# Two transformer-like blocks on one core: weights of the experts split by half chunks in a written order, last tiles and LRU weights rearranged

## The chip, the cores and the metric

The kernel runs on 1 core of one Trainium2 chip. The metric is the device time of one execution in microseconds (us). The core's engines have a queue each and run in order: TensorE (PE; its weight loads are shown as PEld), VectorE (DVE), ScalarE (ACT), GpSimd (POOL), and SyncE (SP), which here issues most DMAs. GpSimd's queue issues the others, all indirect ones among them.

## The reference, cut to what matters

Input x is 1024 tokens by 1024, in float32. A first block (gated mixing, a state-space branch, cross attention) ends in a layer norm. The second block is:

```python
h = rms_norm(x, norm_mix)
lru_in, lru_gate, q, k, v, g_lru, g_attn = split(h @ w_in)
hr = rg_lru(causal_depthwise_conv(lru_in, conv_w, conv_b), ...)   # two block-diagonal gates, a scan over tokens
y_lru = (gelu(lru_gate) * hr) @ w_lru_o
o_attn = diff_attention(q, k, v, cos, sin, ...)   # 8 heads, mask: key chunk of 64 <= query chunk of 64
mixed = sigmoid(g_lru) * y_lru + sigmoid(g_attn) * (o_attn @ w_attn_o)
x = x + mixed @ w_out
x = x + memory_cross_attention_2(x, mem, ...)
x = x + hierarchical_moe(rms_norm(x, norm_ffn), ...)   # 32 experts, top 2 of one group of 8

def expert_block(xb, e):
    gu = xb @ w_gate_up[e]                              # 1024 -> 2 x 512
    return (silu(gu[:, :512]) * gu[:, 512:]) @ w_down[e]  # 512 -> 1024
```

## The kernel before, in words

Every large product is made of three matmuls (`mm3`, lines 174 to 176): each operand is split into a high half in fp32r, copied by ScalarE (`act`, line 154), and a low half, the difference, made by VectorE (`tt`, line 166); `split` does both, and the product is high by high, high by low, low by high. Lines 154, 158, 162, 163 and 166 are helpers that all stages share, so rows are told apart by the names of their tiles.

The order of instructions on each engine is set when the program is built: a scheduler takes them by priority and by the time at which it estimates each to be ready. `high_priority` and `behind` move a block's priority, and `issue_after(i)` keeps a block's instructions on i's engine behind i. A tile of a pool with n buffers waits until the one n allocations before it was last read.

The stages in order, with rough times from the trace:

- The first block (0 to 370 us) and `ln1` (to 465): for 8 tiles of 128 tokens, output product, layer norm, RMS norm, transposes, split into `xnh`, `xnl` (`transpose_split`, line 949). The norm's sum of squares is ScalarE's, its reciprocal roots are GpSimd's (`rsqrt`, line 179). `self.ln_end` holds the last tile's square and scaling; the splits of the memory's transposed input `mh`, `ml` wait for both.
- `lru` (465 to 720): for 8 chunks of 128 channels an input projection (`proj`, tile `pj`, 1024 tokens), a convolution, a gate projection, two small gate products (`pg`), and elementwise work up to a scan. `stream` allocates the split weights (`wh`, `wl`, 4 buffers) and issues load and split right where the projection is traced. `mem2` is a generator that projects the memory's keys and values (`w_ckv`, same 4 buffers) in the gaps; its PSUM pool has one buffer, shared by product and transposes. `attn_const` comes last.
- `attention` (720 to 1440): it begins with the tables `rot` for keys (1) and queries (0), on GpSimd, and the masks `ma`, `mb`. Each query tile and half head has score products (lines 1487, 1488) and one product that adds -2^100 on masked columns (line 1490): ma is 128 by 128, mb 128 by 384, of which 256 columns are used, all fp32r.
- `out_proj` (to 1620) and the mixer (to 1890): output product, memory cross attention as steps s1 to s10 on 8 tiles (`step(n)` works on several tiles at once), routing (`route`). The last tile is alone in its batch: s8 (output product, residual, square), s9 (transposes for the router, then `rows`: x3d and out are written), s10. Between them the first loads of experts' weights are issued as memory comes free (`moe_ahead`): a ring of 1 + 6 + 6 raw buffers (pools RX, RA, RB) of 128 x 4 x 512.
- `moe` (1890 to the end): each expert has 6 chunks of weights of 1 MB, 4 of `w_gu` and 2 of `w_dn`. It takes at most 96 tokens of its list: an indirect load `gather` of rows of 4 KB from x3d into `xg` (3 buffers), transposes and split (`x_parts`), `up` 4 times, `gated`, `a_parts` (transposes and split of the activations), `down` twice, each with a scaling `y` by VectorE, and an indirect `scatter` that adds the rows to out. That is 72 matmuls of 512 columns and 12 transposes an expert. `parts` splits a whole chunk (3 buffers). The loop, lines 2302 to 2325, traces up 0, the activations of the expert before, up 1 and 2, the next expert's `x_parts`, the gather for e + 4, up 3, `gated`, then the two `down` of the expert before and its scatter. `w()` takes the next chunk; from the 78th load on (LIM) the ring no longer uses RB, so it has 7 buffers. A loop for lists over 96 rows stands at the end.

Of the kernel before, what the change touches and what calls it, by code (L numbers as in the profile page):

```python
# [11 lines left out]
F32 = mybir.dt.float32  # L12
# [12 lines left out]
EPS = 1e-6  # L25
# [5 lines left out]
NY = 3  # L31
N0 = 2
CT = 8
NRA, NRB, NRX = 6, 6, 1
OVAT = 8
LIM = 78
# [93 lines left out]
class Model:  # L130
# [37 lines left out]
    def split(self, hi, lo, src, eng=None):  # L168
        self.act(hi, src, AF.Copy)
        self.tt(lo, src, hi.bitcast(F32), OP.subtract, eng)  # L170

    def mm3(self, ps, l, r, start, stop):
        mm = self.nc.tensor.matmul
        mm(ps, l[0], r[0], start=start, stop=False)  # L174
        mm(ps, l[0], r[1], start=False, stop=False)  # L175
        mm(ps, l[1], r[0], start=False, stop=stop)  # L176
# [767 lines left out]
    def transpose_split(self, src, PT, hi, lo):  # L944

        for q in range(2):
# [3 lines left out]
            self.split(hi[:, 4 * q:4 * q + 4], lo[:, 4 * q:4 * q + 4], pt)  # L950
# [6 lines left out]
    def ln1(self):  # L957
# [4 lines left out]
        with self.pool("lnw1") as LW, self.pool("lny", side="right") as NW, self.pool("ln", side="right") as N, self.pool("lnps", bufs=2, space=PSUM) as PO, \  # L962
# [3 lines left out]
            def finish():  # L966
                i, xn = last.pop(0)
                self.transpose_split(xn, PT, self.xnh[:, :, i * 128:(i + 1) * 128],
                                     self.xnl[:, :, i * 128:(i + 1) * 128])
# [18 lines left out]
            for i in range(8):  # L988
# [17 lines left out]
                r = N.tile([128, 2, 512], F32, name="r", tag="r")  # L1006
                st = N.tile([128, 2, 6], F32, name="st", tag="st", bufs=2)
                for n in range(2):
                    self.stt(r[:, n], xr[:, n * 512:(n + 1) * 512], ALPHA, ps[:, n], OP.mult, OP.add)
                    nc.vector.bn_stats(out=st[:, n], in_=r[:, n])  # L1010
                if i < 6:
                    nxx.append(load_x(i + 2))
                mv = N.tile([128, 8], F32, name="mv", tag="mv", bufs=2)
                nc.vector.bn_aggr(out=mv[:, 0:2], in_=st)
                self.ts(mv[:, 2:3], mv[:, 1:2], LN_EPS, OP.add)
                self.rsqrt(mv[:, 3:4], mv[:, 2:3], 1)
                r1 = r.rearrange("p a b -> p (a b)")
                self.ts(r1, r1, mv[:, 0:1], OP.subtract, mv[:, 3:4], OP.mult)
                x1 = N.tile([128, 1024], F32, name="x1t", tag="x1t")
                self.tt(x1, r1, lg, OP.mult)  # L1020
                self.tt(x1, x1, lb, OP.add, nc.vector if i == 7 else nc.gpsimd)
                nc.gpsimd.dma_start(out=self.x1[i], in_=x1)
                xn = N.tile([128, 1024], F32, name="xnt", tag="xnt", bufs=2)
                sq = self.act(xn, x1, AF.Square, accum=mv[:, 4:5])
                self.ts(mv[:, 5:6], mv[:, 4:5], 1.0 / 1024, OP.mult, EPS, OP.add)
                self.rsqrt(mv[:, 6:7], mv[:, 5:6], 1)
                xs = self.stt(xn, x1, mv[:, 6:7], nm, OP.mult, OP.mult)
# [9 lines left out]
    def lru(self):  # L1037
# [9 lines left out]
        with self.pool("lru") as T, self.pool("m2") as M, \  # L1047
                self.pool("pj2", bufs=2, space=PSUM) as PJ, self.pool("pg2", bufs=3, space=PSUM) as PG, \
                self.pool("pm2", bufs=1, space=PSUM) as PM:
            beside = self.mem2(W, M, PM)  # L1050
# [5 lines left out]
            def proj(src, w=None):  # L1056

                w = w or self.stream(W, src, [128, 8, 128])
# [19 lines left out]
            first = [proj(A["w_li"][c], None if c else self.w0) for c in range(2)]  # L1078
# [4 lines left out]
            ahead = next(first[1])  # L1083
            for c in range(8):
                xc = nxt
                if c < 7:
                    nxt = conv(c + 1, ahead if c == 0 else [*proj(A["w_li"][c + 1])][1])
                ps = [*proj(A["w_lgate"][c])][1]
# [11 lines left out]
                for g, t in ((1, ti), (0, tr)):  # L1100
                    for h in range(2):
# [3 lines left out]
                        self.act(t[:, z], p, AF.Tanh, bias=self.hb[:, 2 + 8 * g + c:3 + 8 * g + c], scale=0.5)  # L1105
                next(beside, None)
# [20 lines left out]
            with self.tc.issue_after(self.ln_end[1].ins):  # L1127
                self.attn_const(self.at0)
# [21 lines left out]
    def attn_const(self, T):  # L1150
# [13 lines left out]
        self.sub, self.lamn, self.gcol, self.grow = sub, lamn, gcol, grow  # L1164

    def attention(self):
# [4 lines left out]
        with self.pool("at1") as T1, self.pool("at") as T, \  # L1171
# [3 lines left out]
            sub, lamn, gcol, grow = self.sub, self.lamn, self.gcol, self.grow  # L1175
            rot = {}
            for j in (1, 0):
                t = T1.tile([128, 8, 2, 16], F32, name=f"rot{j}")
                g1 = grow[:, j:j + 1, 0:8].to_broadcast([128, 8, 8])
                g2 = grow[:, j:j + 1, 8:16].to_broadcast([128, 8, 8])  # L1180
                self.tt(t[:, :, 0, 0:8], self.ropec, g1, OP.mult, nc.gpsimd)
                self.tt(t[:, :, 0, 8:16], self.ropes, g1, OP.mult, nc.gpsimd)
                self.tt(t[:, :, 1, 0:8], self.ropes, g2, OP.mult, nc.gpsimd)
                nc.gpsimd.tensor_scalar(out=t[:, :, 1, 0:8], in0=t[:, :, 1, 0:8], scalar1=-1.0, scalar2=None, op0=OP.mult)
                self.tt(t[:, :, 1, 8:16], self.ropec, g2, OP.mult, nc.gpsimd)
                rot[j] = t

            ma = T.tile([128, 128], F32R, name="ma")
            mb = T.tile([128, 384], F32R, name="mb")
            nc.gpsimd.memset(ma.bitcast(F32), 0.0)  # L1190
            nc.gpsimd.memset(mb.bitcast(F32), 0.0)
# [667 lines left out]
    def mixer_tiles(self, x2, XX, xxp, PQ, PT, wcq, wrt, wqp):  # L1859
# [89 lines left out]
        def s8(i, halves=(0, 1)):  # L1949
# [8 lines left out]
            if 1 not in halves:  # L1958
                return
# [525 lines left out]
```

## Time and profile before

| | |
|---|---|
| median of 3 runs | 2520.61 us (2520.1 to 2521.86) |
| profiled execution, its own time | 2518.23 us |
| its span, first to last instruction | 2516.5 us |
| granted TensorE clock, mean | 0.982 |
| PE busy, share of the span | 94% |
| VectorE, ScalarE, GpSimd | 70%, 50%, 20% |
| moved by DMA | 394.29 MB |

The rows come from one profiled execution. Times are us, unless marked ns; L166 is line 166. A matmul's row shows its time through the array with a modelled end; matmuls follow each other more closely than that, so the pace is read from their starts. "Idle before" or a bracket gives the engine's idle time ahead of an instruction and whose end released it.

### The profile page before, as it was taken

What the parts mean: (1) busy time and instruction counts of PE and PEld (TensorE: products, weight loads), DVE (VectorE), ACT (ScalarE), POOL (GpSimd) and SP (SyncE); (2) the same over time, 40 slices, a digit from 0 to 9 for tenths busy, and PEclk for the clock granted to TensorE, in tenths of its full rate; (3) what the DMA queues carried; (4) which work ended last, traced back from release to release, by engine and by line L of the source; (5) the groups of instructions that cost most, each with busy time, mean ns of one, the idle gap of its engine ahead of it and who ended that gap; (6) DMA issues with size and microseconds to landing.
All of it is one profiled execution on the core that took longest, in us unless ns stands there. A gap on an engine that the chain in (4) does not pass through costs nothing. (4 is left out here: it accounts for less than half of the span.)

```text
span 2516.5 us, 34506 instructions
## 1 busy us (share of the span) xinstructions
PE 2364.3 (94%) x13016; PEld 1951.4 (78%) x13016; DVE 1772.8 (70%) x3221; ACT 1246.2 (50%) x1850; POOL 504.8 (20%) x362
## 2 busy tenths in 40 slices
PE   8999989989999999999899899999988999988887
PEld 6888868777889898898798778888876777666665
DVE  9667767676775666666666744236658999988887
ACT  5344532453645545455455522124435777766664
POOL 1011114100021021021121100000002333355542
PEclk9999999999999999999999999999988999999999
DMA  6322353312111111110111466532158998999995
GB/s 222 95 70 63 116 187 115 122 69 91 63 68 55 64 35 40 62 51 34 53 49 40 141 204 220 173 138 80 72 217 308 376 373 306 366 338 336 334 338 183
DMA packets 103834, 394.29 MB, mean 157 GB/s; under 512 B 14129, under 2 KB 33073, under 8 KB 79089
## 3 DMA queue, kind: packets, MB, share of 16 engines
q1 hardware_dynamic: 85008, 335.18, 37.8%
q0 software_dynamic: 18656, 56.88, 7.1%
q8 instruction: 104, 1.70, 0.3%
q14 instruction: 66, 0.53, 0.1%
HBM read 339.07 MB, written 61.31 MB: 159 GB/s over the span
## 5 line engine op out<-in xcount | busy, mean ns | idle before, releaser
L166 DVE TENSOR_TENSOR wl<-raw,wh 128x2048 fp32r<-128x2048 f32 (+2 forms) x310 | 566.0, 1839 | 120.0 <-ACT wh L154 119.6
L154 ACT ACTIVATE wh<-raw 128x2048 fp32r<-128x2048 f32 (+2 forms) x310 | 479.6, 1556 | 290.4 <-PE pj L175 87.3
L2248 POOL DMA_INDIRECT out<-y,lsti x32 | 175.2, 5475 | 331.4 <-DVE y L162 281.3
L175 PE MATMUL pg<-wl,xh 128*96 128x512 f32 x512 | 205.6, 402 | 30.1 <-DVE wl L166 29.9
L174 PE MATMUL pj<-wh,xnh 128*128 128x256 f32 x768 | 221.5, 289 | 3.2 <-ACT pc L154 2.7
L176 PE MATMUL pj<-wh,xnl 128*128 128x256 f32 x768 | 217.7, 284 | 0.0
L175 PE MATMUL pj<-wl,xnh 128*128 128x256 f32 x768 | 217.4, 283 | 0.0
L176 PE MATMUL pg<-wh,xl 128*96 128x512 f32 x512 | 201.7, 394 | 0.0
L174 PE MATMUL pg<-wh,xh 128*96 128x512 f32 x512 | 198.3, 396 | 1.0 <-ACT wh L154 1.0
L174 PEld LDWEIGHTS pj<-wh,xnh 128*128 128x128 f32 x768 | 145.4, 189 | 6.2 <-ACT pc L154 4.8
L175 PEld LDWEIGHTS pj<-wl,xnh 128*128 128x128 f32 x768 | 145.5, 189 | 0.0
L176 PEld LDWEIGHTS pj<-wh,xnl 128*128 128x128 f32 x768 | 145.3, 189 | 0.0
L179 POOL TENSOR_TENSOR ss<-ss,mhalf 128x4 f32<-128x4 f32 (+1 forms) x68 | 74.2, 1092 | 343.6 <-DVE ss L163 254.0
L175 PEld LDWEIGHTS pg<-wl,xh 128*96 128x96 f32 x512 | 82.8, 162 | 76.4 <-DVE wl L166 44.5
L154 ACT ACTIVATE e<-sc,st,ss 128x1024 f32<-128x1024 f32 (+7 forms) x128 | 105.6, 829 | 64.5 <-DVE st L158 47.6
L174 PEld LDWEIGHTS pg<-wh,xh 128*96 128x96 f32 x512 | 82.9, 162 | 37.3 <-ACT wh L154 1.4
L174 PE MATMUL pj<-xnh,wh 128*128 128x512 f32 x256 | 103.4, 405 | 7.3 <-ACT wh L154 7.0
L176 PEld LDWEIGHTS pg<-wh,xl 128*96 128x96 f32 x512 | 83.1, 162 | 32.7
L175 PE MATMUL pj<-xnl,wh 128*128 128x512 f32 x256 | 102.4, 401 | 1.3 <-DVE xnl L166 1.3
L174 PE MATMUL pg<-xnh,wh 128*128 128x512 f32 x256 | 103.1, 403 | 0.4 <-ACT kv L154 0.3
L176 PE MATMUL pj<-xnh,wl 128*128 128x512 f32 x256 | 101.9, 400 | 0.3 <-DVE wl L166 0.3
L176 PE MATMUL pg<-xnh,wl 128*128 128x512 f32 x256 | 102.1, 399 | 0.0
(997 smaller groups left out, 6429.5 us busy)
## 6 DMA issues: line engine op xcount, KB each, us to landing
raw<-in_w_gu SPq DMA_DIRECT2D x128, 1024.0 KB, 7.7
raw<-in_w_dn SPq DMA_DIRECT2D x64, 1024.0 KB, 9.6
raw<-in_w_out SPq DMA_DIRECT2D x16, 512.0 KB, 4.5
ta<-tg POOLq DMA_DIRECT2D x32, 256.0 KB, 2.4
t<-ta SPq DMA_DIRECT2D x14, 512.0 KB, 4.3
raw<-in_w_ga SPq DMA_DIRECT2D x12, 512.0 KB, 3.5
raw<-in_w_v SPq DMA_DIRECT2D x12, 512.0 KB, 3.4
xraw<-in_xT SPq DMA_DIRECT2D x8, 512.0 KB, 8.9
```

What stands on the lines that cost most here:

```text
L154: return self.nc.scalar.activation(out=out, in_=in_, func=func, **kw)
L166: return (eng or self.nc.vector).tensor_tensor(out=out, in0=a, in1=b, op=op)
L174: mm(ps, l[0], r[0], start=start, stop=False)
L175: mm(ps, l[0], r[1], start=False, stop=False)
L176: mm(ps, l[1], r[0], start=False, stop=stop)
L179: self.nc.gpsimd.tensor_tensor(out=out, in0=in_, in1=self.mhalf[:, :w], op=OP.pow)
L2248: return nc.gpsimd.indirect_dma_start(out=self.out, out_offset=bass.IndirectOffsetOnAxis(ap=u["row"], axis=0), in_=u["y"], in_offset=None, ...
```

## The change

It has these parts:

- `ln1`: the last tile's chain gets a high priority; `ln_end` is now the last split, so the splits of the memory's input come behind that.
- `lru`: `proj` takes weights streamed one projection ahead. In `mem2` the two token halves share one PSUM tile, and the transposes use the pool of the gate products. `attn_const` comes in the second of 8 chunks and makes the keys' table and the masks too.
- `unit_qk`: mask operands in bf16, 64 columns.
- Mixer: the gather buffers are filled by GpSimd; the last tile's residual and square go by halves, with a sum of the two squares; its `rows` come behind that sum; `wco` has a pool of its own, left after the last tile's output product, where a pool `moe1` with two more raw buffers and the split buffers opens.
- `moe`: chunks are split by halves (128 x 2 x 512, 4 buffers), each 4 halves ahead of its matmuls. Transposes follow a given matmul; their splits, `gated` and the scalings of y, now ScalarE's, follow a given half's split. LIM is gone: the ring has 15 buffers throughout.

```diff
-NRA, NRB, NRX = 6, 6, 1
+NP = 4
+NRA, NRB, NRX, NRP = 6, 6, 1, 2
-LIM = 78
...
@@ ln1
+                with self.tc.high_priority(URGENT) if i == 7 else nullcontext():
                     r = N.tile([128, 2, 512], F32, name="r", tag="r")
...
-            self.ln_end = sq, xs
             finish()
-            finish()
+            self.ln_end = finish()
...
@@ lru
+            def ahead():
+                if srcs:
+                    ws.append(self.stream(W, srcs.pop(0), [128, 8, 128]))
-            def proj(src, w=None):
-                w = w or self.stream(W, src, [128, 8, 128])
+            def proj(w=None):
+                w = w or ws.pop(0)
+                ahead()
...
+                if c == 1:
+                    with self.tc.issue_after(self.ln_end[1].ins):
+                        self.attn_const(self.at0)
...
@@ attn_const, attention
+        self.rotation(T, 1)
+        self.ma = ma = T.tile([128, 128], BF, name="ma")
+        self.mb = mb = T.tile([128, 64], BF, name="mb")
-            for j in (1, 0):
+            self.rotation(T1, 0)
...
@@ unit_qk
-                    nc.tensor.matmul(base[:, o + n - 256:o + n], ma, mb[:, 128:384] if i == 0 else mb[:, 0:256],
-                                     start=False, stop=True)
+                    end = 128 if i == 0 else o + n
+                    nc.tensor.matmul(base[:, end - 64:end], ma, mb, start=False, stop=True)
...
@@ mem2
-            pt = PS.tile([128, 2, 128], F32, name="pt", tag="pj")
+            pt = PG.tile([128, 2, 128], F32, name="pt", tag="pg")
+            pair = PS.tile([128, 2, 2, 128], F32, name="pj", tag="pj")
-                ps = PS.tile([128, 2, 128], F32, name="pj", tag="pj")
+                ps = pair[:, t]
...
@@ mixer_tiles
+            if len(halves) == 1:
+                n = halves[0]
+                q = slice(512 * n, 512 * n + 512)
+                self.tt(x2[i][:, q], x2[i][:, q], ps[:, n], OP.add)
+                self.act(s[:, q], x2[i][:, q], AF.Square, accum=(rs3[:, i:i + 1], self.ms[:, 0:1])[n])
                 return
...
+                if i == 7 and q:
+                    last = self.tt(rs3[:, 7:8], rs3[:, 7:8], self.ms[:, 0:1], OP.add)
-            rows(i)
+            with tc.issue_after(last.ins) if i == 7 else nullcontext():
+                rows(i)
...
                 s8(7, (1,))
+                wcp.__exit__(None, None, None)
+                self.partsp = self.pool("moe1")
+                self.PARTS = self.partsp.__enter__()
+                self.moe_ahead((self.PARTS, NRP), NRP)
...
-                            nc.vector.memset(t, 0.0)
+                            nc.gpsimd.memset(t, 0.0)
...
@@ moe
-                self.ts(u["y"][:, q], p, u["gate"], OP.mult)
+                self.act(u["y"][:, c * 512:c * 512 + 512], u["pd", c], AF.Copy, scale=u["gate"])
...
+            def ahead(n):
+                if n < len(work):
+                    if n % 2 == 0:
+                        self.moe_ahead()
+                        raws.append(self.moe_raw.pop(0))
+                    ready.append(parts(raws[-1], n % 2))
...
+            for n in range(NP):
+                ahead(n)
+            for n, (f, e, c, k) in enumerate(work):
+                u = U[e]
+                m = f(u, c, k, ready[n][0:2])
+                last = ready[min(n + NP, len(work)) - 1]
+                with tc.issue_after(m.ins):
+                    if f is up and (c, k) == (0, 1) and e > 0:
+                        a_turn(U[e - 1])
+                    if f is up and (c, k) == (1, 1) and e < 31:
+                        x_turn(U[e + 1])
+                with tc.issue_after(last[2].ins), tc.issue_after(last[3].ins):
+                    if f is up and (c, k) == (0, 1) and e > 0:
+                        a_split(U[e - 1])
+                    if f is up and k == 3:
+                        gated(u, c)
+                    if f is up and (c, k) == (1, 1) and e < 31:
+                        x_split(U[e + 1])
+                    if f is down and k == 1:
+                        scaled(u, c)
...
+                ahead(n + NP)
+                if f is up and (c, k) == (1, 1) and e < 28:
+                    with tc.issue_after(put.ins) if e > 1 else nullcontext():
+                        gather(U[e + 4])
+                if f is down and (c, k) == (1, 1):
+                    put = scatter(u)
...
```

`work` lists for each expert its 8 half chunks of `up` and then the 4 half chunks of the expert before's `down`.

## Rows read from the trace of the kernel before

**Rows 1.** Part 1 of the page: busy us, share of the span, instructions of each engine.
```profile
PE 2364.3 (94%) x13016; PEld 1951.4 (78%) x13016; DVE 1772.8 (70%) x3221; ACT 1246.2 (50%) x1850; POOL 504.8 (20%) x362
```
**Rows 2.** Stretches by stage: us, busy (instructions) PE PEld DVE ACT POOL, PEclk, DMA share, GB/s.
```profile
465.00:720.00 255.00, 240.29 (x1122) 197.66 (x1123) 190.97 (x186) 134.19 (x158) 12.80 (x20) 0.97 0.24 81
...
1620.00:1890.00 270.00, 252.50 (x1433) 215.02 (x1431) 144.43 (x325) 102.32 (x205) 18.71 (x21) 0.97 0.35 131
1890.00:2503.00 613.00, 577.21 (x2690) 401.05 (x2690) 554.71 (x444) 416.45 (x323) 251.06 (x62) 0.99 0.94 333
```
**Rows 3.** The same view, two stretches of the MoE between starts of scatters.
```profile
1949.25:2091.32 142.07, 142.07 (x676) 100.30 (x675) 139.16 (x120) 106.42 (x82) 48.93 (x17) 1.00 1.01 374
2200.24:2403.22 202.98, 181.76 (x842) 124.38 (x841) 174.91 (x132) 131.07 (x101) 110.91 (x21) 1.00 0.97 336
```
**Rows 4.** Waits of 2200 to 2400: us in total, times, longest.
```profile
ACT xh L154 <- PE pt L2205: 45.4, 10, 4.5
...
PE pg L175 <- DVE wl L166: 19.6, 19, 1.6
```
**Rows 5.** Timeline of PE at the first and last products of the experts: start, us.
```profile
1896.20 0.90 PE L2205 MATMUL pt<-ident,xg 96*128 96x96 f32 x4 [3.61 <-DMA xg<-x3d,lsti]
...
2502.74 0.39 PE L176 MATMUL pd<-wh,ahl 128*96 128x512 f32 x1
```
**Rows 6.** Groups by form, 2200 to 2400: busy us, mean ns, idle before.
```profile
L166 DVE TENSOR_TENSOR wl<-raw,wh 128x2048 fp32r<-128x2048 f32 x60 | 135.5, 2284 | 16.5 <-ACT wh L154 16.5
L154 ACT ACTIVATE wh<-raw 128x2048 fp32r<-128x2048 f32 x59 | 112.0, 1913 | 8.0 <-PE pg L176 7.6
...
L162 DVE TENSOR_SCALAR y<-pd,lst 96x512 f32<-96x512 f32 x19 | 14.1, 741 | 0.0
```
**Rows 7.** Groups by form, 465 to 720, of VectorE and of ScalarE.
```profile
L166 DVE TENSOR_TENSOR wl<-raw,wh 128x1024 fp32r<-128x1024 f32 x26 | 31.8, 1223 | 35.0 <-ACT wh L154 35.0
...
L154 ACT ACTIVATE wh<-raw 128x1024 fp32r<-128x1024 f32 x26 | 27.4, 1053 | 89.7 <-PE pj L175 78.1 <-issue 7.2 <-DMA raw<-in_w_ckv 4.4
```
**Rows 8.** Part 6 of the page: DMA issues, count, KB each, us to landing.
```profile
raw<-in_w_gu SPq DMA_DIRECT2D x128, 1024.0 KB, 7.7
```
**Rows 9.** Timeline of PE at the end of the norm.
```profile
462.13 1.06 PE L949 MATMUL ptr<-ident,xnt 128*128 128x128 f32 x8 [3.14 <-DVE xnt L158]
...
466.00 0.80 PE L175 MATMUL pj<-xnl,wh 128*128 128x512 f32 x1 [1.28 <-DVE xnl L166]
```
**Rows 10.** The stretch around it; columns as in rows 2.
```profile
460.00:470.00 10.00, 6.28 (x20) 4.54 (x21) 6.42 (x19) 5.40 (x12) 0.75 (x4) 0.66 0.48 155
```
**Rows 11.** Waits of PE, 465 to 720.
```profile
PE pj L174 <- ACT wh L154: 7.0, 4, 3.0
PE pj L174 <- ACT kv L154: 3.3, 2, 1.9
```
**Rows 12.** Timeline of PE at the start of attention.
```profile
728.29 0.66 PE L1249 MATMUL pt<-ident,nr 128*128 128x128 f32 x4 [3.79 <-DVE nr L166]
...
729.01 0.28 PE L176 MATMUL pj<-wh,xnl 128*128 128x256 f32 x1
729.13 0.29 PE L174 MATMUL pj<-wh,xnh 128*128 128x256 f32 x1
```
**Rows 13.** The mask products, by their line: ns min, median, max.
```profile
L1490 PE MATMUL sc<-mb,ma x128: 276/281/415, 777.0 to 1437.4; 128*128 128x256 f32 x128
```
**Rows 14.** Timeline of PE: transposes in attention; bf16 products of the routing.
```profile
907.24 0.60 PE L1558 MATMUL pt<-ident,o 128*128 128x128 f32 x4
...
1873.22 0.18 PE L2095 MATMUL prk<-rt_M,tri 128*128 128x32 bf16 x1
1873.24 0.20 PE L2097 MATMUL prk<-rt_M,one 128*128 128x32 bf16 x2
```
**Rows 15.** Timeline of VectorE in the mixer: the third of three like it.
```profile
1862.42 0.91 DVE L2031 MEMSET xg<- 96x1024 f32 x1 [0.16 <-issue]
```
**Rows 16.** Timeline of PE in the mixer.
```profile
1864.09 1.09 PE L1867 MATMUL ptr<-ident,on 128*128 128x128 f32 x4 [3.53 <-DVE on L166]
```

More of the change, by code (lines that the diff above doesn't have):

```diff
@@ L1075, in conv @@
                 return xc
-            first = [proj(A["w_li"][c], None if c else self.w0) for c in range(2)]
+            first = [proj(None if c else self.w0) for c in range(2)]
             for g in first:
@@ L1082, in lru @@
             self.w0p.__exit__(None, None, None)
-            ahead = next(first[1])
+            second = next(first[1])
             for c in range(8):
@@ L2038, in mixer_tiles @@
         t1p = self.pool("mt8", side="right")
-        with self.pool("wco", side="right") as WC, self.pool("mt7", side="right") as T, \
-                self.pool("po8", space=PSUM) as P2:
+        with self.pool("mt7", side="right") as T, self.pool("po8", space=PSUM) as P2:
+            wcp = self.pool("wco", side="right")
+            WC = wcp.__enter__()
             T1 = t1p.__enter__()
@@ L2205, in x_parts, with x_split @@
                         nc.tensor.transpose(pt[:, a], u["xt"][:, k * 128:(k + 1) * 128], self.ident[0:BLK, 0:BLK])
-                    self.split(u["xh"][:, 4 * q:4 * q + 4], u["xl"][:, 4 * q:4 * q + 4], pt)
-            def up(u, c, k2, raw):
+                    u["px"].append(pt)
+            def x_split(u):
+                u["xh"] = T.tile([128, 8, BLK], F32R, name="xh", tag="xh", bufs=2)
+                u["xl"] = T.tile([128, 8, BLK], F32R, name="xl", tag="xl", bufs=2)
+                for q in range(2):
+                    self.split(u["xh"][:, 4 * q:4 * q + 4], u["xl"][:, 4 * q:4 * q + 4], u["px"][q])
@@ L2224, in a_parts, with gated @@
-            def a_parts(u):
-                pt = PT.tile([128, 4, BLK], F32, name="pt", tag="pt")
+                for k in range(2):
+                    kk = 2 * k2 + k
+                    m = self.mm3(u["pg", c], (u["xh"][:, kk], u["xl"][:, kk]), (ws[0][:, k], ws[1][:, k]),
+                                 kk == 0, kk == 7)
+                return m
+            def gated(u, c):
+                if c == 0:
+                    u["t"] = T.tile([BLK, 512], F32, name="tg", tag="tg", bufs=2)
+                    self.act(u["t"], u["pg", 0], AF.Tanh, scale=u["half"])
+                    self.stt(u["t"], u["t"], 1.0, u["pg", 0], OP.add, OP.mult)
+                else:
+                    self.tt(u["t"], u["t"], u["pg", 1], OP.mult)
@@ L2253, in moe @@
                   "xt": xg[e % 3]} for e in range(32)]
-            def w():
-                if self.raw_n == LIM:
-                    self.ring = [p for p in self.ring if p[0] is not self.RB]
-                self.moe_ahead()
-                return self.moe_raw.pop(0)
             for e in range(3):
                 gather(U[e])
-            x_parts(U[0])
-            gather(U[3])
             def beyond():
@@ L2318, in moe @@
-                if v:
-                    down(v, 0, w())
-                    down(v, 1, w())
-                    put = scatter(v)
-                if e == OVAT:
-                    over = beyond()
-                if e == OVAT + 3:
-                    spread(*over)
+                if e < 32:
+                    work += [(up, e, c, k) for c in range(2) for k in range(4)]
+                if e > 0:
+                    work += [(down, e - 1, c, k) for c in range(2) for k in range(2)]
+            ready, raws = [], []
```

209 lines of the change are left out of this document (103 added, 106 removed).

## The prediction

> **What bounds the kernel now.** I read the busy shares first [rows 1]: TensorE (PE) is busy 94% of the span, so nearly everywhere the time is PE's queue of matmuls plus the holes in it. The stretches by stage [rows 2] say where the holes are: 14.7 us (255 less 240.29) in the LRU, 17.5 us in the mixer, 35.8 us in the experts (MoE), which alone take 613 us. What matters most is the last. One expert is 84 matmuls (72 of 512 columns, 12 transposes). The two stretches of [rows 3] run from one scatter's start to another's: 676 matmuls are 8 experts in 142.07 us, 17.76 us each, with PE busy for all of it; 842 are 10 experts in 202.98 us, 20.30 us each, with PE 90% busy. The same work is 2.54 us per expert slower in the second. So I looked at who waits there [rows 4]: PE waits for VectorE's low halves of the weights (modelled matmul ends hide part of each wait), and ScalarE stands idle 4.5 us per expert before the split of the next tokens, because their transposes are queued on PE behind matmuls whose weights ScalarE has yet to split. No wait of that view is for a landed load. It is an order problem between two in-order queues; in the first stretch the build had put the same instructions in another order.
>
> All sums are against the profiled execution: span 2516.5 us, its own time 2518.23, the runs' median 2520.61, 2.4 above it. What this kernel's measurement can tell from no change is about 0.2%, 5 us.
>
> **Experts, the main term.** The change writes the order out: ScalarE and VectorE split four half chunks ahead of PE, and each transpose goes behind a fixed matmul, its split behind a fixed half chunk. What ScalarE then waits for on PE is something that PE has already passed. PE's work is the same 84 matmuls, so its floor is 17.76 us per expert [rows 3], 32 x 17.76 = 568. The MoE stretch is 613 us for 2690 matmuls, 32 experts [rows 2], of which 6.2 us lie before the last transposes ahead of its first product [rows 5]. 613 - 6 - 568 = 39; 3 us of that I leave at the start, where the clock is still low. **Term: -36.**
>
> Costs put against it. Halving a chunk makes 12 splits of 1024 columns of 6 of 2048: VectorE 2 x 1223 ns against 2284, 0.16 us more per chunk; ScalarE 2 x 1053 against 1913, 0.19 us more [rows 6, 7]. VectorE was busy 139.16/8 = 17.4 us per expert [rows 3]; it gains 6 x 0.16 = 1.0 and loses the two scalings, 2 x 0.741 = 1.5 [rows 6], so 16.9. ScalarE had 106.42/8 = 13.3; plus 1.1 and two scalings of about 0.7 (an estimate, near VectorE's 0.741) makes 15.8. Both stay under 17.76 and hide behind PE, VectorE with under 1 us to spare. If its pieces do not follow each other as closely as now, 18.5 us is my outer value: +24 over the stage.
>
> The ring: a half chunk is 6 matmuls, 17.76/12 = 1.48 us of PE with the transposes' share, four are 5.9; split, subtraction and matmuls of one take 1.05 + 1.22 + 1.48 = 3.8 [rows 7]. Some 2 us are left for the splits of tokens and activations that come between. It fits, not by much.
>
> The loads: at 17.76 us per expert the DMAs moved 374 GB/s [rows 3], 53.1 MB in 142 us. Less gather and scatter (96 rows of 4 KB each way, 0.79 MB per expert, 6.3 in all) that is 46.8 MB, 44.7 loads of 1024 KB [rows 8] where 48 were used: the lead shrinks by 0.42 loads per expert, 13.3 over 32. The old ring begins with 13 loads and goes down to 7; the new one begins with 15 and keeps them. So the two extra buffers are what lets PE's pace last to the end, by under two loads.
>
> A rule that speaks against this: the Trainium skill, DMA: Bandwidth & Descriptors, section Where 436 GB/s comes from, says that for transfers from HBM the HBM side, about 358 GB/s per core, is what binds. The trace of before does not hold to it: 374 GB/s over 142 us. By the page the sum would be, as an estimate, 358 x 17.76 us = 6.36 MB per expert, 0.69 loads short each time, 22 over the stage, 7 more than the lead, some 20 us of the 36 gone.
>
> **Norm tail.** PE waits 3.14 us for the last tile's normalised rows and 1.28 us for their low halves [rows 9]; the clock in that 10 us is 0.66 [rows 10], and the slow matmuls cost some 2.6 us more: 7 in all. Priority for that tile's chain, and the memory's 8 scalings (on ScalarE and VectorE) moved behind the last split, take away what stood in between. Next late is the last split itself, a good 1 us. **Term: -5.5** (0 to -7).
>
> **LRU.** PE waits 7.0 us for ScalarE's weights and 3.3 us for evictions of the memory's single PSUM bank [rows 11]. The weights are late because ScalarE stood 78.1 us before such splits for a buffer that PE held [rows 7] and then had a backlog. One projection of prefetch, and a pair of halves in the bank with the transposes in another pool, aim at both. All idle is 14.7 us, 1.3 of it counted above; the clock, 0.97 over 255 us, costs at most 7.7 more [rows 2]. On SP's queue the loads move ahead of the gate and memory weights, each of which is issued well before its use. Bounds 0 and -21; I take a bit over half, since ScalarE's order stays the build's. **Term: -12.**
>
> **Attention.** The first transposes wait 3.79 us for the rotated keys [rows 12], whose tables GpSimd makes only then. They move into the LRU, with the masks; GpSimd was busy 12.8 of 255 us there [rows 2]. The queries' table stays. **Term: -3** (0 to -5, the clock after the gap included). The mask matmul, 128 of them [rows 13], goes from 256 columns to 64 in bf16. Matmuls of 256 columns stand 0.12 us apart [rows 12]. Below that there are two rows: bf16 matmuls 0.02 us apart, and f32 transposes of 128 columns 0.11 apart, each with weights of its own to load [rows 14]. What follows a mask is f32 with 128 columns of weights, so I take 0.11: 128 x 0.01 = **-1.3**; the other end is 128 x 0.1 = -13.
>
> **Mixer's end.** Three fills of the gather buffers, 0.91 us each [rows 15] and a gap, stand on VectorE ahead of the last tile's scaling, and PE waits 3.53 us for that [rows 16]. On GpSimd they hide: its queue is empty there (2.9). The last tile in halves starts its residual sum and square half a tile earlier, 0.6 us on VectorE and 0.5 on ScalarE, and the write of its rows goes behind the route's sum (1.5 together). PE then waits 3.61 us for the second expert's tokens before its first product [rows 5]; the new order puts them behind the sixth half chunk (3.6). The gathers still leave GpSimd in the same order, and the first one sets the start. **Term: -8** (-3 to -11). The tail after the last matmul, 2502.7 to 2516.5 [rows 5], stays: the last scatter still waits for the one before.
>
> **Sum.** 36 + 5.5 + 12 + 3 + 1.3 + 8 = 65.8. 2518.2 - 65.8 = 2452.4 in a profiled execution, 2455 in the median.
>
> **Rivals.** *Loads bound the experts.* If 374 GB/s does not hold over the whole stage, the lead runs out. At 355, half way to the second stretch's 336 [rows 3], an expert's (6.29 + 0.79) MB take 19.9 us; the 177 loads behind the lead take 177/6 x 19.9 = 588 us, 20 more than PE: 2475. For it: the DMA share is 0.97 to 1.01 in both stretches. Against: in the slow one no split waits for a load, so 336 is what was asked for. Chance 0.13. The page's cap is this rival.
>
> *VectorE or the ring bounds.* 18.5 us per expert, +24: 2479. For it: VectorE at 16.9 of 17.76. Against: the first stretch ran with 17.4. Chance 0.12.
>
> *The change doesn't order what it says.* The build still chooses by its own clock inside the limits set, the experts stay at their pace, norm and LRU too; 1.3 + 3 + 8 and two loads of lead, 2 x 142/44.7 = 6, are left: 2502. Chance 0.06. With norm and LRU alone unmoved it is 2472, in the range.
>
> *GpSimd bounds: slower.* Scatter and gather took 48.93/8 = 6.1 us of GpSimd per expert in the first stretch and 110.91/10 = 11.1 in the second [rows 3], where the longer ones fall on VectorE's back-to-back subtractions. Cut in halves, these may leave no gap. If each of the two then takes 11 us, 22 us per expert, the stage is 32 x 22 = 704 against 607, +97; with the other 30 us of gain it is +67: 2588. It decides from (607 + 30)/32 = 19.9 us per expert. Against: VectorE was 98% busy in the first stretch, where GpSimd took 6.1. Chance 0.05. The Trainium skill, GPSIMD Engine Reference, section Key points, says that GpSimd shares its SBUF interfaces with VectorE and contends with VectorE instructions of two SBUF inputs, as the subtractions are; the growth of these rows agrees.
>
> My forecast has 0.62; 0.02 is for no change.
>
> **Numbers.** Predicted 2455. Low: the LRU at its end (-9), masks three quarters of the way (-9), mixer and norm at theirs (-5), attention's start (-2): 2430. High: the rivals of 0.13 and 0.12 reach 2479, 2486 with half of the LRU's 12 us missing. Faster by over 0.2%: 0.92; within: 0.02; slower: 0.06.
>
> **What would show it.** Scatters 17.8 us apart to the end, ScalarE's wait for the token transposes gone, PE near 99% busy in the MoE: the main term. A split that waits for a landed load: the first rival. VectorE's subtractions back to back and PE waiting for them: the second. Scatters of 8 us and more: the last. No wait of 3 us at the last norm tile, at attention's first transposes and at the first expert: the small terms. The prediction is wrong if the experts stay at 20 us, or if attention, whose order the build may shuffle, moves by more than 5 us.

## The result, and the profile after

The changed kernel takes 2487.0 us in the median of four runs (2483.3 to 2491.2), the kernel before 2521.2 beside it: a ratio of 0.987 (0.986 to 0.988). It is faster, as forecast, by 34 us and not by 66: 2487 lies just above the range given (2430 to 2486). The profiled execution took 2485.6 us, its span 2483.9.

First the busy shares (part 1 of the page; [rows 1] before), then stretches of the changed kernel: from the last normalised transposes to attention's first gates, 9 experts between two starts of scatters, and from the experts' first product to their last. Columns as in [rows 2].

```profile
PE 2355.6 (95%) x13016; PEld 1936.7 (78%) x13016; DVE 1748.2 (70%) x3344; ACT 1314.5 (53%) x2102; POOL 341.5 (14%) x363
...
460.45:683.40 222.95, 218.08 (x1016) 180.33 (x1016) 173.06 (x182) 126.10 (x152) 8.85 (x17) 0.98 0.24 78
...
1932.66:2091.41 158.75, 158.75 (x757) 113.17 (x756) 149.73 (x177) 136.24 (x162) 29.40 (x18) 1.00 1.02 375
...
1883.38:2473.15 589.77, 570.56 (x2683) 401.79 (x2682) 532.81 (x564) 484.55 (x570) 86.81 (x60) 1.00 0.93 339
```

TensorE's busy time fell only by 9 us; what fell is its idle time. Nine experts run at 158.75/9 = 17.64 us each with TensorE never idle, the pace that [rows 3] showed for the first experts of before. Over the whole stage 589.77 - 570.56 = 19.2 us are idle: the pace was not kept. The waits of the same stretch say on whom (us in total, times, longest):

```profile
PE pd L173 <- ACT y L154: 16.6, 12, 1.7
PE pg L175 <- DVE xl L166: 1.6, 3, 0.7
PE pg L173 <- ACT xh L154: 0.9, 1, 0.9
```

VectorE's low halves, 19.6 us in 200 before [rows 4], are gone from this list. In their place stands `y`, the scaling of a finished half of the output, which the change moved to ScalarE.

To see where the 34 us come from I cut every profile at the same instructions of TensorE. In us:

| stretch, from one mark to the next | before | after | after + places (first run below) | + early weights, two late (sixth) |
|---|---|---|---|---|
| start to last normalised transposes | 463.2 | 460.5 | 463.2 | 462.4 |
| to attention's first gates (LRU) | 237.0 | 223.0 | 220.5 | 220.4 |
| to the first key transposes | 28.1 | 25.4 | 25.4 | 25.4 |
| to attention's last output transposes | 727.0 | 728.6 | 730.6 | 730.4 |
| to the mixer's first query product | 245.0 | 245.2 | 245.2 | 245.3 |
| to its first output transposes | 21.9 | 27.2 | 27.0 | 21.9 |
| to the last tile's ranks | 161.6 | 162.2 | 162.3 | 159.0 |
| to the experts' first product | 13.1 | 11.3 | 11.7 | 10.1 |
| to their last product | 606.3 | 589.8 | 567.2 | 567.1 |
| to the end of the span | 13.4 | 10.7 | 10.4 | 10.3 |

The first and the fourth row vary by some us between profiles that differ elsewhere only (460.5 to 464.5; 725.6 to 733.0 over all of them), so a difference of 3 us there can't be put down to the change. In the first row of before, a wait of 2.17 us was followed by a granted clock of 0.94 over 30 us; after, the same wait (2.15) by 1.00.

### The profile page after: what moved, and what is told of

It is laid out like the page before. It is cut to its first block, busy times and chain, and to the rows that moved or that the text cites. A ratio compares the mean times of both kernels' runs of the same rounds, so it can differ in the third digit from the quotient of the medians.

```text
span 2483.9 us, 35045 instructions
## 1 busy us (share of the span) xinstructions
PE 2355.6 (95%) x13016; PEld 1936.7 (78%) x13016; DVE 1748.2 (70%) x3344; ACT 1314.5 (53%) x2102; POOL 341.5 (14%) x363
## 5 line engine op out<-in xcount | busy, mean ns | idle before, releaser
L166 DVE TENSOR_TENSOR wl<-raw,wh 128x1024 fp32r<-128x1024 f32 (+1 forms) x496 | 587.7, 1209 | 130.3 <-ACT wh L154 126.1
L154 ACT ACTIVATE wh<-raw 128x1024 fp32r<-128x1024 f32 (+1 forms) x496 | 512.1, 1048 | 250.0 <-PE pj L174 67.2
L173 PE MATMUL pd<-wh,ah 128*96 128x512 f32 x248 | 98.2, 400 | 16.6 <-ACT y L154 16.6
L174 PE MATMUL pg<-xnl,wh 128*128 128x512 f32 x256 | 102.2, 399 | 0.0
```

The source lines that it names most:

```text
L154: return self.nc.scalar.activation(out=out, in_=in_, func=func, **kw)
L166: return (eng or self.nc.vector).tensor_tensor(out=out, in0=a, in1=b, op=op)
```

## The experiments

Theory after the first reading: two losses ate the gain. In the experts the order gives each small piece a lower place (what it must stand behind) but no upper one (what must stand behind it), and from the 12th expert on the build put the scalings behind the next expert's splits. In the mixer, weights came late at its start and early splits stood in the last tile's way. The rivals for the experts are those of the prediction: the loads, or VectorE.

This is ScalarE's timeline in the changed kernel (start, us busy, instruction, in brackets its idle time and what ended it), one expert at the full pace and then one late:

```profile
2032.46 2.22 ACT L154 ACTIVATE wh<-raw 128x1024 fp32r<-128x1024 f32 x2 [0.55 <-PE pg L175]
2035.01 0.69 ACT L154 ACTIVATE y<-pd,lst 96x512 f32<-96x512 f32 x1 [0.33 <-PE pd L175]
2035.60 2.00 ACT L154 ACTIVATE wh<-raw 128x1024 fp32r<-128x1024 f32 x2
2038.01 0.69 ACT L154 ACTIVATE y<-pd,lst 96x512 f32<-96x512 f32 x1 [0.42 <-PE pd L175]
...
2139.91 1.06 ACT L154 ACTIVATE wh<-raw 128x1024 fp32r<-128x1024 f32 x1 [0.32 <-PE pg L175]
2140.88 1.24 ACT L154 ACTIVATE y<-pd,lst 96x512 f32<-96x512 f32 x2
2143.27 1.06 ACT L154 ACTIVATE wh<-raw 128x1024 fp32r<-128x1024 f32 x1 [1.15 <-PE pd L175]
```

And TensorE at the second place:

```profile
2141.60 0.48 PE L173 MATMUL pd<-wh,ah 128*96 128x512 f32 x1 [1.72 <-ACT y L154]
```

In the first, each scaling waits for its product (0.33 and 0.42 us) and runs at once. In the second, both of one expert come together, the earlier eleven half chunks late, behind the splits for the next expert's down products. Those need a bank of `pd`, there are two, and both are full until the scalings ran: TensorE stands 1.72 us. It does so in 8 of the later experts and for less in 4 more, 16.6 us in all; some late scalings cost it nothing.

**Upper places in the experts.** `due` gathers what a step's small pieces return, and the split after the next may not pass it:

```
+                    with ExitStack() as pins:
+                        for p in held:
+                            pins.enter_context(tc.issue_after(p.ins))
+                        ready.append(parts(raws[-1], n % 2))
...
-                        scaled(u, c)
+                        due += scaled(u, c)
...
                 ahead(n + NP)
+                held, due = due, []
```

> The changed kernel, but each small piece of ScalarE and VectorE in the experts (the split of the tokens, of the activations, the tanh, the scaling of an output half) gets an upper place as well: the split of the half chunk after the next one may not pass it. Theory: from about the 12th expert on the build put the scalings up to 11 half chunks late, and TensorE stood 1.72 us per expert before a PSUM bank that they had to free. Then the time from the first expert's first product to the last (589.8 us in the changed kernel) becomes 566 to 573, scatters 17.6 to 17.8 us apart to the end, no wait of TensorE on the scaling, about 2466 in all. Rival, VectorE or the ring of four half chunks is the bound: at most 5 us less, TensorE then waits for the low halves. Rival, the loads: TensorE's pace holds only until the lead of 15 loads is used up, and splits wait for landed loads after that; about 580.

Measured: 2466.5 us, ratio 0.979 (0.977 to 0.981). The experts' stretch, and the only two waits of TensorE in it:

```profile
1885.85:2453.08 567.23, 566.91 (x2683) 402.65 (x2682) 526.54 (x564) 480.97 (x570) 90.90 (x60) 1.00 0.96 352
...
PE pd L173 <- ACT ahl L154: 0.2, 1, 0.2
PE pg L174 <- DVE wl L166: 0.2, 1, 0.2
```

The theory's numbers. Both rivals fall: with the same splits, VectorE's work nearly the same (526.5 us, 532.8 in the changed kernel) and the same loads, the experts run at TensorE's pace from end to end. The run bounds all small pieces at once; that the scaling is the one that cost is read from the waits (16.6 of the 19.2 us).

**Low halves behind the list.** The first four subtractions wait for the last tile's list:

```
+            with tc.issue_after(self.listed.ins):
+                for n in range(NP):
+                    ahead(n)
```

> The changed kernel, but the first four half chunks' subtractions on VectorE stand behind the last tile's list (the cast to integers that the gathers read). Theory: in the changed kernel these four (4.8 us on VectorE) stood in front of the last tile's sum and rows, and the three weight loads that they let go (1 MB each) were in front of the rows' write, so the first gather left 3.2 us after its list was there. Without them TensorE's wait of 7.0 us at the last ranks becomes about 2 to 3, the gather leaves within 1 us of its list, and the first gather stands 6 to 8 us earlier against the last tile's output product; the run is 5 to 7 us shorter. Rival: the gather waits for something else (the fills of its buffers, GpSimd), then only the 4 us at the ranks come back, or the subtractions now stand before the first expert's products, and nothing is gained.

This is what it starts from, in the changed kernel: VectorE, then SP's queue, GpSimd and TensorE.

```profile
1862.58 2.35 DVE L166 TENSOR_TENSOR wl<-raw,wh 128x1024 fp32r<-128x1024 f32 x2
1864.98 1.22 DVE L166 TENSOR_TENSOR wl<-raw,wh 128x1024 fp32r<-128x1024 f32 x1
1866.12 0.15 DVE L166 TENSOR_TENSOR rs<-rs,ms 128x1 f32<-128x1 f32 x1
...
1863.82 2.73 SPq L2187 DMA_DIRECT2D raw<-in_w_dn  x2
1867.53 0.33 SPq L2187 DMA_DIRECT2D raw<-in_w_gu  x1
...
1867.70 0.59 POOL L1991 DMA_DIRECT2D x3d<-h  x1 [18.58 <-DVE rs L163]
1877.68 1.10 POOL L2215 DMA_INDIRECT xg<-x3d,lsti  x1 [8.77 <-issue]
...
1871.82 0.19 PE L2126 MATMUL prk<-rt_M,tri 128*128 128x32 bf16 x1 [7.00 <-DVE rt_M L166]
```

Measured: 2496.9 us, 10 more than the changed kernel. In this run:

```profile
1872.27 4.62 DVE L166 TENSOR_TENSOR wl<-raw,wh 128x1024 fp32r<-128x1024 f32 x4
...
1873.49 4.37 POOL L2215 DMA_INDIRECT xg<-x3d,lsti  x1 [6.70 <-DVE wl L166]
...
1869.70 0.19 PE L2126 MATMUL prk<-rt_M,tri 128*128 128x32 bf16 x1 [5.00 <-DVE rt_M L166]
...
1884.22 0.58 PE L2232 MATMUL pt<-ident,xg 96*128 96x96 f32 x2 [11.12 <-DMA xg<-x3d,lsti]
```

Half the theory holds: the wait at the ranks is 2 us shorter, and the gather leaves 1.1 us after its list (1872.35) and not 3.2 (1874.48 to 1877.68). But beside four subtractions in a row its issue takes 4.37 us, not 1.10, and two loads that they let go (1874.6 and 1876.9) run with it: its rows come 10.7 us after the issue's start, 4.2 in the changed kernel. That makes the way from the ranks to the first product 4.5 us longer. The greater part of the 10 us lies in the experts, which took 598.8 us; TensorE's wait on `y` was 19.6 us there, in 15 experts, as the build had put other scalings late.

**Cross output weights early.**

```
-    wco.append(self.load_w(WC, ..., f"wco{k}", (WC, "wr", 2)))
+    wco.append(self.load_w(WC, ..., f"wco{k}", (T, "hs"[k % 2], 1)))
```

> The changed kernel, but the raw buffers of the cross output weights lie in the two row buffers of the tile pool again and not in the pool that closes early. Theory: their place in memory came free only when the residuals were done, so the first two loads left 18 us later against the first query product than before, ScalarE stood 2.7 us before the third one with the exponentials behind it, TensorE stood 2.0 us and its clock fell to 0.6 for some 9 us: 5.4 us lost between the first query product and the first output product of the mixer. With the loads early that stretch goes from 27.2 back to 21.9 us, 4 to 6 us shorter in all. Rival: the stretch got longer by the order of ScalarE's instructions, and the loads were late but covered: no more than 1 us.

In the changed kernel, SP's queue, then ScalarE, TensorE, and the stretch behind (columns as in [rows 2]); the last line is SP's queue in this run:

```profile
1682.77 0.33 SPq L2187 DMA_DIRECT2D raw<-in_w_gu  x1
1683.19 12.40 SPq L1622 DMA_DIRECT2D raw<-in_w_co  x4
...
1696.55 1.06 ACT L154 ACTIVATE wco2h<-raw 128x1024 fp32r<-128x1024 f32 x1 [2.74 <-DMA raw<-in_w_co]
1697.52 0.55 ACT L154 ACTIVATE e<-sc,st 128x256 f32<-128x256 f32 x1
...
1702.25 0.58 PE L1954 MATMUL po<-v,ph 128*128 128x256 f32 x1 [1.97 <-ACT ph L154]
...
1701.00:1710.00 9.00, 7.16 (x34) 6.70 (x35) 5.88 (x9) 2.38 (x5) 1.01 (x1) 0.62 0.00 0
...
1680.60 0.81 SPq L1622 DMA_DIRECT2D raw<-in_w_co  x2
```

Measured: 2479.3 us, ratio 0.984 (0.982 to 0.986). The stretch is 21.88 us, as before the change (21.86); the loads leave 5.3 us ahead of the first query product, 0.6 behind it in the changed kernel. So the late loads cost 5.4 us, of which the waits on TensorE are 2.4, with the granted clock at 0.62 from 1701 to 1710. The last tile's ranks came 2.6 us earlier against the first output transposes too (159.6 us, 162.2 in the changed kernel), which was not expected: 1.2 us of it is a shorter wait there (0.43 us for 1.61), the rest the granted clock, 1.00 for 0.88 over the last tile's output products.

**Scaling on VectorE.** `scaled` as before the change: `self.ts(..., u["pd", c], u["gate"], OP.mult)`.

> The changed kernel, but the two scalings of an expert's output stay on VectorE, as before the change. Theory (order): VectorE's queue holds them near their place, so TensorE does not wait for a PSUM bank; but VectorE then has 16.7 + 1.5 = 18.1 us of work per expert, and the experts take 580 to 592 us, about the 589.8 of the changed kernel. Rival (ScalarE has too much with the scalings): the experts go to TensorE's 17.7 us, 568, some 20 us shorter.

Measured: 2503.4 us; experts 603.4 us. Both expectations miss. TensorE's waits in the experts, and what became of the scatters on GpSimd (min, median and max ns):

```profile
PE pd L173 <- DVE y L162: 23.5, 10, 3.6
...
L2290 POOL DMA_INDIRECT out<-y,lsti x31: 1403/3270/17687, 1913.8 to 2479.6; - x31
```

The scaling slips on VectorE's queue too, and the experts take longer than in any run that has it on ScalarE. So the slip does not come from the engine that was chosen, and without an upper place ScalarE was the better home; VectorE with an upper place was not run.

**Places and weights together.** The edits of the first and the third run.

> The upper places in the experts and the early cross output weights together. Theory: two separate losses, so their gains add up: the experts 567 us from first to last product as with the places alone, the mixer's stretch 21.9 us as with the weights alone, 2466.5 less 7 to 8: 2458 to 2460. Rival: with the experts at full pace the loads' lead is the limit and an earlier start only moves the wait; then not below 2464.

Measured: 2457.5 us, ratio 0.973 (0.971 to 0.975); experts 567.0 us, the mixer's stretch 21.86. The gains add up, to half a us less than the 2458 expected at the least.

**Two of four late.** With both, and the first half chunks split so:

```
+            x0 = x_split(U[0])
             for n in range(NP):
+                with tc.issue_after(x0[1].ins) if n > 1 else nullcontext():
+                    ahead(n)
```

> The kernel with both, and of the first four half chunks' subtractions two stay ahead of the last tile's list and two go behind the first expert's token splits. Theory: GpSimd's issue of the first gather took 4.4 us beside four subtractions in a row and 1.1 without any, and loads let go by a subtraction delay the rows' write or the gathers; with two early the sum of the last tile comes 2.4 us earlier, one load instead of three stands in front of the rows' write, and no subtraction lies beside the gathers. The first expert's token transposes, 9.7 us behind the last ranks with the weights early, come at 7 to 8, the ranks themselves 2 us earlier; the first expert then waits up to 2 us for low halves; 2 to 5 us shorter than without. Rival: the loads that are let go later are missing at the end, where the lead is down to some 5 us: not shorter.

Measured: 2454.8 us, ratio 0.973 (0.971 to 0.974): the shortest here, though the intervals of this and the last do not tell them apart. In its profile:

```profile
1864.57 0.18 PE L2126 MATMUL prk<-rt_M,tri 128*128 128x32 bf16 x1 [5.00 <-DVE rt_M L166]
...
1869.16 1.10 POOL L2215 DMA_INDIRECT xg<-x3d,lsti  x1 [7.51 <-DVE ovr L2307]
...
1873.44 1.54 PE L2232 MATMUL pt<-ident,xg 96*128 96x96 f32 x8 [4.98 <-DMA xg<-x3d,lsti]
```

The wait at the ranks is 2 us shorter, the issue 1.10 us, the first token transposes 8.66 us behind the ranks where the run before had 9.48 (7 to 8 were expected), and there is no wait for low halves. But the ranks themselves are only 0.6 us earlier against the first query product, not 2: from the last tile's first output transposes to its router products the granted clock was 0.87 here and 1.00 in the run before, and that stretch took 1.3 us longer. From the first query product to the experts' first the gain is 1.4 us.

**LRU: one part undone at a time, then both.** Each projection loads its own weights (`if not w: ahead(); w = ws.pop(0)`); the memory's halves take turns in one slot (`ps = PS.tile([128, 2, 128], ...)`, the transposes in `PS` again); both.

> The changed kernel, but in the LRU each projection loads its own weights when it is emitted, not one ahead. Theory: the 14 us that the LRU gained come from the weights being split in time; then most of it is lost: the time from the last normalised transposes to attention's first gates goes from 220 to 223 us to 230 or more. Rival: the gain comes from the memory's pair of halves in its PSUM bank; then it stays within 3 us.

> The changed kernel, but the memory's two halves share one PSUM tile slot one after the other again, with the transposes in the same pool. Theory: the memory's evictions cost TensorE 3 us in all before the change and some of it still does, so 1 to 4 us more than the 220 to 223 between the last normalised transposes and attention's first gates. Rival: this carries the LRU's gain, then 8 us or more.

> The changed kernel with both of the LRU's parts undone: no projection loaded ahead, and no pair of halves in the memory's bank. Theory: each of the two alone takes the waits for ScalarE away, since each gives its queue room; with both gone the 14 us come back, the stretch from the last normalised transposes to attention's first gates goes from 220 to 223 us to 232 or more. Rival: neither was it, the gain comes from what else moved (the memory's scalings behind the last split, the tables into GpSimd's idle time): then it stays below 226.

Measured in one run each (2491.8, 2487.6 and 2503.3 us in all), from the last normalised transposes to attention's first gates: 221.7, 222.6 and 232.4 us (223.0 in the changed kernel, 237.0 before; 220.0 to 223.6 over the ten profiles that have both parts). TensorE's waits in that stretch, of the run with both undone:

```profile
PE pj L173 <- ACT wh L154: 4.4, 3, 2.5
PE pj L173 <- ACT kv L154: 3.3, 2, 1.9
PE pj L175 <- DVE wl L166: 2.1, 2, 1.8
```

The seventh run's theory falls, and so do the eighth's theory and its rival: either part alone is enough. The ninth's theory holds: with neither, the waits of [rows 11] are back, the first in part (4.4 us of 7.0), the second whole, and some 10 of the 14 us. The rest goes with parts not tried alone (the tables' place, the memory's scalings).

**Mask back, priority off.** The mask product of before (256 columns, full type); and `with nullcontext():` where the last normalised tile had priority.

> The changed kernel with the mask product of 256 columns in the matmul's full type again, and its tiles filled when attention begins. Theory: a mask product of 64 columns takes 0.04 us where one of 256 took 0.12, but what stands behind it comes no earlier, so attention (first transposes to last output transposes, 728 to 733 us in the runs so far) stays within 3 us of that. Rival: the mask saves 128 x 0.08 = 10 us and a worse order elsewhere takes them; then 738 or more.

> The changed kernel without the priority for the last normalised tile. Theory: the tile's chain is a chain of dependences on VectorE and GpSimd in which the same weight subtractions stand with and without it; TensorE's wait of 3.3 us before its last normalised transposes stays within 0.5 us. Rival: the priority does order it and the wait is what is left: then 5 us or more.

Measured in one run each (2495.0 and 2483.3 us in all): attention 733.3 us with the old mask (725.6 to 733.0 over the runs with the new one), and a wait of 3.31 us without the priority, 3.31 with it. Neither part shows. Of the mask the timeline of TensorE in the changed kernel says why:

```profile
757.55 0.28 PE L1505 MATMUL sc<-kl,qs 128*128 128x256 f32 x1
757.68 0.20 PE L1509 MATMUL sc<-mb,ma 128*128 128x64 bf16 x1
757.72 0.36 PE L1504 MATMUL sc<-kh,qs 128*128 128x256 f32 x1
757.92 0.28 PE L1505 MATMUL sc<-kl,qs 128*128 128x256 f32 x1
```

The product behind the mask starts 0.04 us after it, but the next one 0.20 after that, where 0.12 is usual [rows 12]: what the mask gave, its follower takes. Over the 54 mask products of the changed kernel that have score products on both sides and no wait, the two steps are 0.04 and 0.26 us in the median, where the kernel before had 0.12 and 0.18: the same sum.

**Thirteen buffers.** The kernel with the upper places, without the line that adds two raw buffers.

> The kernel with the upper places in the experts, but with 13 raw buffers and not 15. Theory: at full pace the loads come in at 368 to 375 GB/s and fall behind TensorE's use, so the lead is what carries the stage; with 15 its smallest value was 5 to 6 us near load 167. Two loads fewer are 5.7 us less, the lead is just used up near the end, and the experts take 567 to 571 us. Rival: the lead is not what counts, the loads follow the use: no change of the smallest lead.

Measured: 2472.2 us in its one run; experts 574.3 us, 7.1 more than with 15, 3 over the most that was expected. ScalarE's waits for landed loads in the experts, of this run and then of the one with 15:

```profile
ACT wh L154 <- DMA raw<-in_w_gu: 11.6, 14, 1.9
ACT wh L154 <- DMA raw<-in_w_dn: 5.7, 7, 1.5
```

```profile
ACT wh L154 <- DMA raw<-in_w_dn: 1.1, 2, 0.7
ACT wh L154 <- DMA raw<-in_w_gu: 1.1, 3, 0.5
```

At 17.7 us per expert the lead does run down (with 15 buffers, from landing to the first split, 28.3 us at load 47, 5.0 at load 143 and 0.1 at load 167, counted from 0), and the two buffers just carry it to the end: ScalarE waits 2.2 us for loads in all, and TensorE none.

## Why the prediction was wrong where it was

**Experts (-36 forecast, -16.6 measured).** The floor was right: 17.76 forecast, and 567 us from first product to last once the order is kept, against 568. So were the costs put against it (VectorE 149.73/9 = 16.6 us per expert at full pace, 16.9 forecast; the ring fits; the two buffers carry the loads). The step that failed is "The change writes the order out". What it writes is what each piece must stand behind, and nothing that must stand behind the piece. The rival "doesn't order what it says" had the mechanism, but as all or nothing, with 0.06. It came out in part: full pace for the first twelve experts, up to 1.72 us lost in a dozen later ones. How many is luck of the build: in the eight profiles where the scaling stays on ScalarE and nothing bounds it from above, the stretch took 588.4 to 598.8 us, though most of their edits lie elsewhere. With the upper places it took 567.0 to 567.2 in three.

**The loads.** The rival asked whether 374 GB/s holds over the whole stage. It nearly does: with the upper places the DMAs moved 370 and 368 GB/s (2000 to 2200, 2200 to 2400), and with 13 buffers, where ScalarE does wait for loads, 371 (2300 to 2390). The cap named beside the rival was 358 GB/s per core for transfers from HBM, from the Trainium skill (DMA: Bandwidth & Descriptors, section Where 436 GB/s comes from), which has it as a stack's 716 GB/s over two cores. On the one core of this kernel the measurements stand against it.

**Mixer (-8 forecast, +4.3 measured from the first query product to the experts' first).** Three costs were missing. The first: I followed the pool that closes early to what it lets in, not to what its move in memory makes late: +5.4 at the mixer's start. The second: I let the sum of the last tile come "half a tile earlier" and did not count the four subtractions that the changed order puts ahead of it (4.8 us on VectorE). They are 2.0 of the 7.0 us that TensorE waits at the ranks, as the second run shows; what the other 5.0 stand on was not tried. The third: I wrote that "The gathers still leave GpSimd in the same order", which is true, but not what the rows that they read wait for: three loads of 1 MB, free by the early splits, left SP's queue ahead of the write. That write landed 3.3 us after its issue in the kernel before (1876.28 to 1879.54) and 9.1 in the run with upper places (1869.85 to 1878.90), which has the same three loads ahead of it; there the first gather left 1.0 us after the landing. What I had counted came: the wait of [rows 16] went from 3.53 to 1.61, and the second wait of [rows 5] is gone (token transposes to first product 1.48 us, 5.76 before). With the repairs of the sixth run the stretch is 5.5 us shorter than before, of the 8 forecast.

**Norm tail (-5.5 forecast, about 1 measured).** The wait is 3.31 us, not gone. "Priority for that tile's chain" takes nothing away: VectorE does the same pieces in the same order without it. Two weight subtractions among them run in gaps where the chain waits for GpSimd or ScalarE (449.11 and 455.16), but two other pieces stand in its way, a subtraction of weights and the low halves of the tile before. VectorE in the changed kernel, each with the step of the chain behind it:

```profile
447.95 1.17 DVE L166 TENSOR_TENSOR wl<-raw,wh 128x1024 fp32r<-128x1024 f32 x1
449.04 0.15 DVE L162 TENSOR_SCALAR mv<-mv 128x1 f32<-128x1 f32 x1
...
452.76 1.28 DVE L166 TENSOR_TENSOR xnl<-ptr,xnh 128x512 fp32r<-128x512 f32 x2
453.96 1.21 DVE L166 TENSOR_TENSOR x1t<-x1t,row_ln_b 128x1024 f32<-128x1024 f32 x1
```

What the wait would be without these two was not tried. The second wait (1.28) is gone. In the kernel before, VectorE did five of the memory's scalings (463.28 to 465.34) right ahead of that split; that their move did it was not tried alone.

**LRU (-12 forecast, -14.0 measured), attention's start (-3, -2.7).** Right in size, and the 14.0 contain the norm tail's second wait, which lies behind the mark. For the LRU I had taken the two parts as two gains, and they are one, got by either.

**Mask (-1.3).** Nothing to be told from the scatter of attention, as a value near nothing and not the other end, 13, had it; the places in the timeline say nothing was gained.

**GpSimd as the bound (2588).** The other way round: scatters of before took 175.2 us in all in the experts, after 47.5. With it went 2.6 us of the tail behind the last product, which I had left as it was: the last scatter but one took 1.46 us of GpSimd and not 3.41, and the last waits for it.

**The sum.** The forecast's upper end is 2479 and half of 12, which is 2485 and not 2486. The sixth run's 2454.8 us is the forecast's 2455, but of another kernel and in part by luck: against before its experts are 39.2 us shorter (36 forecast), its LRU 16.6 (12), its mixer 5.5 (8) and its tail 3.1 (nothing), while the norm's first row is 0.8 shorter (5.5) and attention 3.5 longer, both within their scatter.

## What to carry to other kernels

An instruction that is only told what to stand behind has no place: where the order matters, bound each small piece from both sides, and look in the timeline at a late repetition of a loop as well as an early one. When a buffer is freed earlier or lies elsewhere, ask which load that lets go and whose transfer stands behind it in the queues. Two repairs that each clear the same wait are one gain.

## What the runs showed of the hardware

GpSimd's indirect transfers took longer where VectorE had more to do beside them. A scatter took 5475 ns in the mean before the change, 1483 after, with the scaling on ScalarE, and 3553 with it back on VectorE (175.2, 47.5 and 113.7 us for 32); the first gather's issue took 1.10 us alone and 4.37 beside four subtractions. In the kernel before, the second and third gather took 2.25 and 1.86 us beside subtractions (VectorE from 1887.39 to 1894.09), in the changed kernel 0.99 and 0.96 with VectorE idle. The Trainium skill, GPSIMD Engine Reference, section Key points, says that GpSimd shares its SBUF interfaces with VectorE and that instructions of VectorE with two SBUF inputs contend with it; the subtractions are such, and the gathers agree with it. No run separates how the scatters hang on the moment at which the scaling lets them go.

A short wait is dear where the granted clock falls with it: around and behind waits of 1.97 and 0.41 us in the mixer it was 0.62 over 9 us, most of them at the lower of its two levels (1.2 GHz, the upper is 2.4), and the stretch lost 5.4 us.

Open: with all repairs TensorE still waits 5.0 us at the last ranks and 5.0 for the first tokens, and 3.3 at the end of the norm. Moving the write of the last rows ahead of the loads by hand was not tried.
